# Opening of a two-block transformer kernel: inputs loaded first, modulation and first convolution group in pairs of K-blocks, modulation sums in halves

## The chip, the cores and the metric

The program runs on one core of one Trainium2 chip. The metric is the device time of one execution in microseconds, taken as a median over runs. The engines are TensorE (PE, with its weight loads as PEld), VectorE (DVE), ScalarE (ACT), GpSimd (POOL), and SyncE (SP), whose queue issues the loads from memory.

## The reference

Two transformer blocks of two layers each run one after the other on a sequence of 256 tokens of width 1024, in 32-bit floats. The change is in the first layer of the first block. There a modulation vector is computed from a conditioning vector, for the tokens (`c`) and for a context of 256 rows (`c_ctx`), then the normalised tokens are scaled and shifted by it and go through a short convolution:

```python
mod = jax.nn.silu(c) @ w_ada[i] + b_ada[i]
mod_c = jax.nn.silu(c_ctx) @ w_ada[i] + b_ada[i]
sh1, sc1, g1, sh2, sc2, g2 = jnp.split(mod[:, None, :], 6, axis=-1)
...
h = _modulate(_rms_norm(x, norm_mix[i]), sh1, sc1)
hc = _modulate(_rms_norm(ctx, norm_mix[i]), sh1c, sc1c)
...
b_gate, c_gate, u = jnp.split(h @ w_in, 3, axis=-1)
z = c_gate * u
...
zc = sum(conv_w[j] * zp[:, j:j + n] for j in range(CONV_WIDTH))
return (b_gate * zc) @ w_out
```

`_modulate(h, shift, scale)` is `h * (1 + scale) + shift`. `w_ada` has 6 pieces of 1024 columns for each layer. The shift and the scale of the first normalisation (pieces 0 and 1) are needed before the first matmul of the convolution, piece 2 after it, and pieces 3 and 4 ahead of the feed-forward net.

## The kernel before, in words

Activations lie transposed, 1024 features as 8 K-blocks of 128 partitions, and tokens and context side by side as 512 columns. To keep 32-bit precision on a faster matmul type, every operand is split into a high part and a rest, and a product is three matmuls (`mm3`, L240 to L245): high by high, high by rest, rest by high. ACT writes the high part of a weight (L106) and DVE the rest (L107).

All weights come through one stream (`WeightStream`, L57): a list of units of at most 128 x 1024 elements, loaded in order by SP (L90) into five raw buffers, split two units ahead of use into four pairs of buffers. A load can only start when the unit five places ahead in the list has left its buffer. Units marked raw are not split but used as they are.

Engines take instructions in their program order. A scheduler fixes that order when the program is built, with its own estimate of durations, so an instruction that waits holds all that stands behind it on its engine.

The opening (`conv_block`) does this. Sums of squares of the tokens (X) and of the context (C) give a reciprocal root by Newton steps (`diagonal`, L347 to L786), which is spread over partitions by a matmul with ones (L791); `normalise` writes `xr` (L793). The shift and scale pieces are computed in four chunks of 512 columns, each over all 8 K-blocks: two with raw weights (`ada_direct`, matmul L454, row copy L459, transposes L440) and two with split weights (`ada_fast`, matmuls L417 and L418, row copy L423, transposes L427). Chunks 0 and 2 hold the first halves of shift and scale. With them `modulate(0)` (L802, then split at L251 and L252) makes K-blocks 0 to 3 of the convolution's input, and the first convolution matmuls (L243 to L245) run on them; the other two chunks give K-blocks 4 to 7.

The convolution has four groups g of 256 features, each with three products c, u and b of 48 K-block steps, that is 144 matmuls of 512 columns. A group's results are combined by DVE and ACT (L853 to L861). Meanwhile the later modulation pieces run on DVE: each unit of 128 x 1024 weights is multiplied by the conditioning value of its partition and added to an accumulator, once for the tokens and once for the context (L473, L475). After 8 units a piece is summed over partitions: PE transposes the accumulators into auxiliary PSUM banks (L483), DVE reduces each bank (L485). There are three auxiliary banks, and a piece for two vectors needs four. `ADA_UNITS` says how many units are taken at which step.

Of the kernel before, what the change touches and what calls it, by code (L numbers as in the profile page):

```python
# [140 lines left out]
def ada_units(w, j, raw):  # L141
    return cols_units(w, j * 512, 512, list(range(8)), raw)


# [21 lines left out]
class Net:  # L166
    def __init__(self, tc, a, out, es):
# [11 lines left out]
        self.banks(5, 3)  # L179
# [3 lines left out]
        nc.sync.dma_start(self.kc, a["consts"])  # L183
# [5 lines left out]
        self.X = self.cp.tile([P, KB, T], F32, name="X")  # L189
        self.mod = self.cp.tile([P, 2, 48, 2], F32, name="mod")  # L190
        self.modA = self.cp.tile([P, 4, KB, 2], F32, name="modA")


# [203 lines left out]
    def ada_start(self):  # L397
        nc = self.nc
        sil = self.sil = self.cp.tile([P, 16], F32, name="sil")
        self.ada_plan = AdaPlan()  # L400
        self.ada_pending = []
        nc.scalar.activation(sil, self.pk[:, 0:16], AF.Silu)
# [5 lines left out]
    def ada_fast(self, layer, j):  # L408
# [3 lines left out]
        done = 0  # L412
        while done < KB:
            hi, lo, nk, _ = self.ws.take()
            for kk in range(nk):
                kb = done + kk
                nc.tensor.matmul(ps[0:4, :], self.c4[:, kb, :], hi[:, kk, :], start=kb == 0, stop=False)  # L417
                nc.tensor.matmul(ps[0:4, :], self.c4[:, kb, :], lo[:, kk, :], start=False, stop=kb == KB - 1)  # L418
            done += nk
            if done < KB:  # L420
                yield
        row = self.tmp()
        nc.scalar.copy(row[0:4, :], ps[0:4, :])  # L423
        yield
        pt = self.aux_bank()
        for b in range(4):
            nc.tensor.transpose(pt[:, 4 * b : 4 * b + 4], row[0:4, b * P : (b + 1) * P], self.ident[0:4, 0:4])  # L427
        m = self.mod[:, layer, 4 * j : 4 * j + 4, :]
        bias = self.p(f"b_ada{layer}")[:, 4 * j : 4 * j + 4, None].to_broadcast([P, 4, 2])
        col = self.small(16, "ada_col")  # L430
        nc.vector.tensor_copy(col, pt[:, :16])
        cv = col.rearrange("p (b v s) -> p b v s", b=4, v=2)
        nc.vector.tensor_tensor(m, cv[:, :, :, 0], cv[:, :, :, 1], ALU.add)
        nc.vector.tensor_tensor(m, m, bias, ALU.add)

    def ada_columns(self, layer, j, row):

        pt = self.aux_bank()
        for b in range(4):
            self.nc.tensor.transpose(pt[:, 2 * b : 2 * b + 2], row[0:2, b * P : (b + 1) * P], self.ident[0:2, 0:2])  # L440
        bias = self.p(f"b_ada{layer}")[:, 4 * j : 4 * j + 4, None].to_broadcast([P, 4, 2])
        m = self.mod[:, layer, 4 * j : 4 * j + 4, :]
        self.nc.vector.tensor_tensor(m, pt[:, :8].rearrange("p (b v) -> p b v", b=4), bias, ALU.add)

    def ada_direct(self, layer, j):

        nc = self.nc
        ps = self.aux_bank()
        sil = self.sil.rearrange("p (v k) -> p k v", v=2)
        done = 0  # L450
        while done < KB:
            w, _, nk, _ = self.ws.take()
            for kk in range(nk):
                nc.tensor.matmul(ps[0:2, :], sil[:, done + kk, :], w[:, kk, :], start=done + kk == 0, stop=done + kk == KB - 1)  # L454
            done += nk
            if done < KB:
                yield
        row = self.tmp()
        nc.scalar.copy(row[0:2, :], ps[0:2, :])  # L459
        yield  # L460
        self.ada_columns(layer, j, row)

    def ada_slow(self, layer, j, vecs):
# [13 lines left out]
        yield  # L477
        col = self.small(16, "ada_sum")
        for v in range(vecs):
            for h in range(2):  # L480
# [4 lines left out]
                nc.vector.tensor_reduce(col[:, o : o + 4], pt.rearrange("p (b k) -> p b k", b=4), AX.X, ALU.add)  # L485
        bias = self.p(f"b_ada{layer}")[:, 8 * j : 8 * j + 8, None].to_broadcast([P, 8, vecs])
        nc.vector.tensor_tensor(self.mod[:, layer, 8 * j : 8 * j + 8, 0:vecs], col[:, : 8 * vecs].rearrange("p (v b) -> p b v", b=8), bias, ALU.add)

    def ada_at(self, *step):
        self.ada_pending = [g for g in self.ada_pending if next(g, WAIT) is None]  # L490
        for layer, j, kb in self.ada_plan.at(step):
            if kb == 0:
                self.ada_piece = self.ada_slow(layer, j, ada_vecs(layer, j))
            next(self.ada_piece)
            if kb == KB - 1:
                self.ada_pending.append(self.ada_piece)

    def ada_flush(self):
        for g in self.ada_pending:
            for _ in g:  # L500
                pass
        self.ada_pending = []

    def mod_scale(self, layer, which, half):

        nv = 2 - layer * which
        hs = slice(4 * half, 4 * half + 4)
        g = self.p(("norm_mix" if which == 0 else "norm_ffn") + str(layer))[:, hs, None].to_broadcast([P, 4, nv])
        sc = self.mod[:, layer, (3 * which + 1) * 8 + 4 * half : (3 * which + 1) * 8 + 4 * half + 4, 0:nv]
# [161 lines left out]
ADA_FIRST = (0, 2, 1, 3)  # L671
ADA_DIRECT = (0, 2)
# [26 lines left out]
def stream_specs(a):  # L699
# [3 lines left out]
    for i in range(2):  # L703
        s += ada_units(w[0], ADA_FIRST[i], ADA_FIRST[i] in ADA_DIRECT)
    for k0 in (0, 4):
        for c0 in (1024, 2048):
            s += cols_units(a["conv_w_in"], c0, 256, k8[k0 : k0 + 4])
# [1238 lines left out]
```

## Time and profile before

| what | before |
|---|---|
| median of 3 runs | 2047.08 us (2044.90 to 2047.14) |
| the profiled execution | 2047.39 us, span 2045.6 us, mean granted clock 0.995 |
| PE busy | 2009.8 us, 98% of the span |
| DVE busy | 1497.8 us, 73% |
| ACT busy | 1026.5 us, 50% |
| memory read | 345.68 MB, 170 GB/s over the span |

Times within the execution are microseconds from the start of the span. A row of the timeline gives start, duration, engine, source line, operation, tiles written and read, how many instructions were merged, and in brackets how long the engine was idle before and what ended that. Successive matmuls overlap in the records, so what a matmul costs is the distance between two starts, not its duration. One matmul in 32-bit floats shows as two records. A row of windows gives the stretch, its length, busy time with the count of instructions for PE, PEld, DVE, ACT and POOL, then the granted clock of PE, the busy share of the DMA engines and GB/s; where only one tile's or one line's instructions are asked for, engines that have none are left out.

### The profile page before, as it was taken

How to read it: one execution, taken by the hardware profiler on the slowest of the kernel's cores; microseconds unless marked ns; L12 is line 12 of the kernel's file. 1: busy time of each engine (PE TensorE's matmuls, PEld its weight loads, DVE VectorE, ACT ScalarE, POOL GpSimd, SP SyncE). 2: the span in 40 equal slices, each digit the busy share in tenths (PEclk: the TensorE clock that was granted, in tenths of full speed). 3: DMA queues.
4: the chain of work that ended last, by engine and by line, in shares of the span. 5: the costliest groups of instructions: out<-in, count | busy, mean ns of one | idle time of the engine just before them, and what ended most of it. 6: DMA issues, size and time to landing. Idle time of an engine off the chain costs nothing. (4 is left out here: it accounts for less than half of the span.)

```text
span 2045.6 us, 31905 instructions
## 1 busy us (share of the span) xinstructions
PE 2009.8 (98%) x12318; PEld 1769.8 (87%) x12318; DVE 1497.8 (73%) x2632; ACT 1026.5 (50%) x1684; POOL 4.1 (0%) x24
## 2 busy tenths in 40 slices
PE   7999999999999999999999999999999999999999
PEld 3778988888899999888888899998888888989888
DVE  5996777777577779766677767787767776887764
ACT  4432533223355556655455546655545554675552
POOL 0000000000000000000000000000000000000000
PEclk8999999999999999999999999999999999999999
DMA  7773365577454334565566564556556656425554
GB/s 242 237 215 120 118 190 180 170 235 248 126 178 133 91 98 131 155 188 187 181 187 194 177 189 126 158 171 194 181 185 191 190 180 186 135 83 171 186 180 134
DMA packets 315080, 348.82 MB, mean 171 GB/s; under 512 B 12528, under 2 KB 299376, under 8 KB 314928
## 3 DMA queue, kind: packets, MB, share of 16 engines
q1 hardware_dynamic: 314928, 346.78, 54.9%
q8 instruction: 97, 1.59, 0.3%
q14 instruction: 55, 0.45, 0.1%
HBM read 345.68 MB, written 1.05 MB: 170 GB/s over the span
## 5 line engine op out<-in xcount | busy, mean ns | idle before, releaser
L106 ACT CAST whi<-wraw 128x512 fp32r<-128x512 f32 (+1 forms) x777 | 608.2, 804 | 738.8 <-issue 192.4
L107 DVE TENSOR_TENSOR wlo<-wraw,whi 128x512 fp32r<-128x512 f32 (+1 forms) x777 | 702.0, 918 | 366.3 <-ACT whi L106 362.0
L306 PE MATMUL pg<-x,whi 128*128 128x512 f32 x1408 | 386.9, 396 | 0.5 <-DVE x L255 0.4
L306 PEld LDWEIGHTS pg<-x,whi 128*128 128x128 f32 x1408 | 239.5, 188 | 34.2 <-DVE x L255 2.2
L306 PE MATMUL po<-s,whi 128*128 128x512 f32 x880 | 243.0, 394 | 0.0
L308 PEld LDWEIGHTS pg<-x,wlo 128*128 128x128 f32 x1408 | 213.9, 188 | 32.4
L308 PE MATMUL pg<-x,wlo 128*128 128x256 f32 x1408 | 221.0, 279 | 0.0
L243 PE MATMUL pm<-xh,whi 128*128 128x512 f32 (+1 forms) x576 | 218.3, 382 | 0.8 <-ACT xh L251 0.8
L244 PE MATMUL pm<-xl,whi 128*128 128x512 f32 (+1 forms) x576 | 219.0, 381 | 0.0
L245 PE MATMUL pm<-xh,wlo 128*128 128x512 f32 (+1 forms) x576 | 218.5, 380 | 0.0
L475 DVE SCALAR_TENSOR_TENSOR ada_acc<-wraw,sil,ada_acc 128x1024 f32<-128x1024 f32 x112 | 140.6, 1280 | 33.5 <-DMA wraw<-in_w_ada 33.1
L306 PEld LDWEIGHTS po<-s,whi 128*128 128x128 f32 x880 | 148.7, 189 | 18.1
L308 PEld LDWEIGHTS po<-s,wlo 128*128 128x128 f32 x880 | 137.5, 188 | 20.5
L308 PE MATMUL po<-s,wlo 128*128 128x256 f32 x880 | 142.5, 280 | 0.0
L243 PEld LDWEIGHTS pm<-xh,whi 128*128 128x128 f32 x576 | 109.3, 190 | 21.9 <-ACT xh L251 1.5
L245 PEld LDWEIGHTS pm<-xh,wlo 128*128 128x128 f32 x576 | 109.3, 190 | 20.8
L244 PEld LDWEIGHTS pm<-xl,whi 128*128 128x128 f32 x576 | 109.3, 190 | 20.4 <-issue 0.2
L243 PE MATMUL pm<-sh,whi 128*128 128x256 f32 (+1 forms) x352 | 113.8, 323 | 0.0
L245 PE MATMUL pm<-sh,wlo 128*128 128x256 f32 (+1 forms) x352 | 113.6, 323 | 0.0
L244 PE MATMUL pm<-sl,whi 128*128 128x256 f32 (+1 forms) x352 | 113.3, 322 | 0.0
L245 PE MATMUL pm<-whi,xl 128*128 128x256 f32 x352 | 99.6, 283 | 0.0
L306 PE MATMUL pg<-xh,whi 128*128 128x512 f32 x352 | 96.1, 394 | 1.9 <-DVE xh L252 1.9
(431 smaller groups left out, 3390.5 us busy)
## 6 DMA issues: line engine op xcount, KB each, us to landing
wraw<-in_ffn_w_in SPq DMA_DIRECT2D x264, 512.0 KB, 3.6
wraw<-in_ffn_w_out SPq DMA_DIRECT2D x128, 512.0 KB, 3.6
wraw<-in_w_ada SPq DMA_DIRECT2D x96, 512.0 KB, 4.5
wraw<-in_a_w_in SPq DMA_DIRECT2D x28, 512.0 KB, 3.8
wraw<-in_conv_w_in SPq DMA_DIRECT2D x24, 512.0 KB, 4.7
wraw<-in_attn_w_qkv SPq DMA_DIRECT2D x24, 512.0 KB, 4.0
wraw<-in_ffn_w_out SPq DMA_DIRECT2D x28, 256.0 KB, 2.9
wraw<-in_b_w_in SPq DMA_DIRECT2D x14, 512.0 KB, 3.9
```

Source lines behind the costliest of these rows:

```text
L106: self.nc.scalar.copy(hi[:, cs], raw[:, cs])
L107: self.nc.vector.tensor_tensor(lo[:, cs], raw[:, cs], hi[:, cs].bitcast(F32), ALU.subtract)
L243: mm(ps, ah, bh, start=first, stop=False)
L244: mm(ps, ah, bl, start=False, stop=False)
L245: mm(ps, al, bh, start=False, stop=last)
L306: self.nc.tensor.matmul(pss[c], hi[:, kk, cs], x2[:, done + kk], start=done + kk == 0, stop=False)
L308: self.nc.tensor.matmul(pss[c][:, 0, :], lo[:, kk, cs], x2[:, done + kk, 0, :], start=False, stop=done + kk == nblocks - 1)
L475: nc.vector.scalar_tensor_tensor(accs[v], w, c, accs[v], ALU.mult, ALU.add)
```

## The change

- **Loads.** X is loaded second, right behind the small parameters (`pack`), then C, then the constants, then five units of the weight stream. Before, the constants came first and two weight units stood between X and C.
- **Statistics.** Tokens and context share one run of the Newton steps (4 columns at once). Squares are taken in turn by ACT and DVE, and their sums over partitions are accumulated by small matmuls as they come.
- **Added matmuls.** 28 matmuls of ones by a constant (`warm`), whose results are not used, stand ahead of and between the statistics.
- **Chunks.** A chunk i now holds 256 columns of the shift and 256 of the scale, for K-blocks 2i and 2i+1 alone (`ada_parts`). Chunks 0 and 1 use raw weights, 2 and 3 split ones; the total of columns is the same.
- **First convolution group.** It runs by pairs of K-blocks: for each pair, c, u and b one after the other, into six open PSUM banks (six main and two auxiliary banks up to here, then five and three as before). The weights of this group come in units of 128 x 512 instead of 128 x 1024. Chunk i+1 is computed behind c of pair i, its transposes stand between the two halves of u, and the modulation of the next pair follows.
- **Units and sums.** The four units of later modulation pieces that ran with group 0 are gone from there, group 3 ends with one unit instead of two, and five now run with the output projection of the convolution (`conv_out`). A piece's sum is taken at most two banks at a step and two or more steps after its last unit.

```diff
-        self.banks(5, 3)
+        self.banks(6, 2)
...
     def ada_at(self, *step):
-        self.ada_pending = [g for g in self.ada_pending if next(g, WAIT) is None]
+
+        self.ada_step += 1
+        for _ in range(2):
+            if self.ada_pending and self.ada_pending[0][0] <= self.ada_step - 2:
+                self.ada_sum()
...
-ADA_UNITS = {("conv", 0, 2): 4}
-ADA_UNITS.update({("conv", g, n): 3 if n == 2 and g < 3 else 2 for g in range(1, 4) for n in range(3)})
+ADA_UNITS = {("conv", g, n): 3 if n == 2 else 2 for g in range(1, 4) for n in range(3)}
+ADA_UNITS["conv", 3, 2] = 1
+ADA_UNITS.update({("conv_out", g): 3 - g for g in range(2)})
...
+    ada = [[u for c1 in (0, 1024) for u in cols_units(w[0], c1 + i * 256, 256, k8, i < ADA_RAW)] for i in range(4)]
+    s += ada[0]
+    for i in range(4):
+        for n, c0 in enumerate(CONV_COLS):
+            s += cols_units(a["conv_w_in"], c0, 256, k8[2 * i : 2 * i + 2])
+            if n == 0 and i < 3:
+                s += ada[i + 1]
...
+    net.load_halves(net.X, net.a["xT"])
     net.load_halves(net.C, net.a["ctxT"])
+    nc.sync.dma_start(net.kc, net.a["consts"])
+    net.ws.load(5)
+    pcu = [[net.main_bank() for _ in range(2)] for _ in CONV_COLS]
+    warm(16)
+    dg = diagonals()
...
+    for i in range(4):
+        ada = None
+        for n, pss in enumerate(pcu):
+            hi, lo, nk, _ = net.ws.take()
+            for c in range(2):
...
+                    net.mm3(pss[c], hi[:, kk, cs], lo[:, kk, cs], xh[:, kb, :], xl[:, kb, :], kb == 0, kb == KB - 1)
+                if n == 1 and c == 0 and ada is not None:
+                    for _ in ada:
+                        pass
+                    modulate(i + 1)
+            if n == 0 and i < 3:
+                ada = net.ada_parts(i + 1)
+                for _ in range(3):
+                    next(ada)
```

Three places in the built order matter to the prediction.

First, PE at the opening. Before (whi and wlo are the two parts of a weight, xh and xl those of the convolution's input, pa an auxiliary and pm a main PSUM bank, kc the constants, c_104 the split conditioning vector): all of the raw chunks (L454) stand ahead of the first convolution matmul (L243).

```order
L454 MATMUL pa<-wraw,sil 2x512 x4
L791 MATMUL pa<-t,ones 128x256
L361 MATMUL pa<-mean,acc 128x1 x4
L454 MATMUL pa<-wraw,sil 2x512 x4
L791 MATMUL pa<-t,ones 128x256
L454 MATMUL pa<-wraw,sil 2x512 x8
L440 MATMUL pa<-kc,t 128x2 x8
L417 MATMUL pa<-whi,c_104 4x512
L418 MATMUL pa<-wlo,c_104 4x512
L417 MATMUL pa<-whi,c_104 4x512
L418 MATMUL pa<-wlo,c_104 4x512
L243 MATMUL pm<-xh,whi 128x512 x4
```

The same place now (a raw chunk's matmul is L429 and has 256 columns, its transposes are L439, the convolution is L242 to L244, L849 spreads the reciprocal root):

```order
L429 MATMUL pa<-wraw,sil 2x256 x8
L849 MATMUL pa<-t,ones 128x256 x2
L429 MATMUL pa<-wraw,sil 2x256 x8
L439 MATMUL pa<-kc,t 128x2 x4
L429 MATMUL pa<-wraw,sil 2x256 x7
L242 MATMUL pm<-xh,whi 128x512 x2
L429 MATMUL pa<-wraw,sil 2x256
L243 MATMUL pm<-xl,whi 128x512
```

One chunk with its transposes, and seven matmuls of the next, now stand ahead of the first convolution matmul; the second half of that next chunk (8 more L429) follows after the 12 matmuls of c of the first pair, then come 6 of u, the four transposes of chunk 1, and the other 6 of u.

Second, ACT at the second modulation. Before, behind the first raw chunk's row copy:

```order
L459 COPY t<-pa 2x512
L106 CAST whi<-wraw 128x512 x5
L459 COPY t<-pa 2x512
L106 CAST whi<-wraw 128x512
L802 ACTIVATE t<-xr,mod,modA 128x256 x3
```

Now, behind the first chunk's row copy (L435; L853 keeps the reciprocal root, L833 scales and shifts):

```order
L106 CAST whi<-wraw 128x512
L853 COPY acc<-pa 128x512
L435 COPY t<-pa 2x512
L833 ACTIVATE t<-xr,mod,modA 128x256 x2
L250 CAST xh<-t 128x512 x2
L106 CAST whi<-wraw 128x512 x5
L435 COPY t<-pa 2x512
L833 ACTIVATE t<-xr,mod,modA 128x256 x3
```

Five weight casts stand ahead of the row copy of chunk 1 as they stood ahead of the second row copy before. By the numbers of the buffers the last two of the five are the two halves of one unit of 128 x 1024, the first unit of chunk 2.

Third, PE at a piece's sum. Before, in group 2 of the convolution, twelve transposes (three banks), four matmuls, and four transposes (the fourth bank):

```order
L483 MATMUL pa<-kc,ada_acc 128x128 x12
L243 MATMUL pm<-xh,whi 128x512
L244 MATMUL pm<-xl,whi 128x512
L245 MATMUL pm<-xh,wlo 128x512
L243 MATMUL pm<-xh,whi 128x512
L483 MATMUL pa<-kc,ada_acc 128x128 x4
L244 MATMUL pm<-xl,whi 128x512
```

Now the same piece's sum stands in two places, each of eight transposes (two banks), 48 convolution matmuls apart; the first of them:

```order
L244 MATMUL pm<-xh,wlo 128x512
L470 MATMUL pa<-kc,ada_acc 128x128 x8
L242 MATMUL pm<-xh,whi 128x512
```

A sum of the first feed-forward net that stood as 12, one matmul, 4 (around 350 us) is split in the same way. The sum late in `conv_out` (now 12, one matmul, 4; before 12, two matmuls, 4) and the two sums during the feed-forward output (12, two matmuls, 4) keep that form. From the feed-forward net's first output on, the order on every engine is the same as before.

More of the change, by code (lines that the diff above doesn't have):

```diff
@@ L776, in units, with warm @@
+    def warm(n):
         for _ in range(n):
[L777 to L794 removed]
@@ L887, in conv_block @@
+        conv_pool.close()
         state = {}
```

333 lines of the change are left out of this document (170 added, 163 removed).

## The prediction

> **What bounds the kernel now.** I read the page first, then the windows of the opening, then the timeline of PE, and last that of ACT and DVE around PE's gaps.
>
> ```profile
> PE 2009.8 (98%) x12318; PEld 1769.8 (87%) x12318; DVE 1497.8 (73%) x2632; ACT 1026.5 (50%) x1684; POOL 4.1 (0%) x24
> ```
>
> PE is busy 98% of the span, so a gain must come from the 2% in which it is idle or from time in which it works slowly. The windows (PE, PEld, DVE, ACT, POOL, then granted clock, DMA share, GB/s) show where both lie:
>
> ```profile
> 0.00:20.00 20.00, 9.24 (x28) 4.06 (x29) 10.14 (x31) 6.40 (x12) 0.20 (x4) 1.00 0.88 292
> 20.00:40.00 20.00, 15.55 (x43) 4.85 (x42) 11.57 (x31) 8.72 (x17) 0.00 (x0) 0.84 0.80 258
> ...
> 12.00:14.00 2.00, 2.00 (x5) 0.75 (x6) 1.13 (x7) 1.15 (x2) 0.00 (x0) 1.00 1.08 372
> ...
> 34.00:36.00 2.00, 1.34 (x7) 0.71 (x7) 1.38 (x4) 1.38 (x4) 0.00 (x0) 0.50 0.94 314
> ...
> 38.00:40.00 2.00, 2.00 (x5) 1.61 (x6) 1.19 (x2) 2.00 (x5) 0.00 (x0) 0.50 0.81 298
> ...
> 42.00:44.00 2.00, 2.00 (x7) 1.55 (x6) 2.00 (x4) 1.94 (x4) 0.00 (x0) 0.52 0.04 8
> ...
> 130.00:132.00 2.00, 2.00 (x6) 1.51 (x6) 2.00 (x5) 0.00 (x0) 0.00 (x0) 0.50 0.78 237
> ```
>
> PE lacks 10.8 us of the first 20 and 4.5 of the next, and from 34 to 44 it runs at a clock of 0.5. PE's timeline gives the chain:
>
> ```profile
> 10.76 1.86 PE L361 MATMUL pa<-mean,acc 128*128 128x1 f32 x8 [10.76 <-DVE acc L352]
> ...
> 24.60 7.03 PE L454 MATMUL pa<-wraw,sil 128*2 128x512 f32 x16
> ...
> 34.66 0.58 PE L440 MATMUL pa<-kc,t 2*128 2x2 f32 x4 [2.70 <-ACT t L459]
> ...
> 37.88 2.07 PE L243 MATMUL pm<-xh,whi 128*128 128x512 f32 x4 [0.84 <-ACT xh L251]
> ...
> 129.00 0.91 PE L483 MATMUL pa<-kc,ada_acc 128*128 128x128 f32 x4 [1.92 <-DVE ada_sum L485]
> ...
> 350.31 0.66 PE L483 MATMUL pa<-kc,ada_acc 128*128 128x128 f32 x4 [1.68 <-DVE ada_sum L485]
> ```
>
> The convolution starts at 37.88. The gap of 2.70 ahead of the transposes (L440) is ACT's doing, as its timeline shows:
>
> ```profile
> 33.51 0.62 ACT L106 CAST whi<-wraw 128x512 fp32r<-128x512 f32 x1 [1.33 <-DMA wraw<-in_w_ada]
> 34.04 0.57 ACT L459 COPY t<-pa 2x512 f32<-2x512 f32 x1
> ```
>
> The row copy's input was there when the raw chunk ended (31.6), but a cast that waited for its load stood ahead of it. When group 0 ends is read from a count, the tile pm alone (PE, PEld, DVE, ACT):
>
> ```profile
> 0.00:80.95 80.95, 37.65 (x144) 28.94 (x145) 1.15 (x2) 1.17 (x2) 0.94 0.76 247
> 81.00:124.40 43.40, 43.40 (x193) 35.95 (x192) 4.10 (x7) 1.75 (x3) 1.00 0.69 216
> ```
>
> The 144th convolution matmul starts by 80.95, and behind it 192 to 193 take 43.40 us, 0.226 each, without a hole. So E, the end of group 0, is the point to forecast; what E gains, the whole kernel gains, as long as PE stays full behind it.
>
> **Part by part: inputs first.** The loads' rows on ACT, and two of the page's rows on time to landing:
>
> ```profile
> 8.55 1.15 ACT L347 ACTIVATE t<-X 128x512 f32<-128x512 f32 x2 [0.28 <-DMA X<-in_xT]
> ...
> 14.18 1.15 ACT L347 ACTIVATE t<-C 128x512 f32<-128x512 f32 x2 [0.34 <-DMA C<-in_ctxT]
> ```
>
> ```profile
> wraw<-in_ffn_w_out SPq DMA_DIRECT2D x128, 512.0 KB, 3.6
> wraw<-in_w_ada SPq DMA_DIRECT2D x96, 512.0 KB, 4.5
> ...
> wraw<-in_ffn_w_out SPq DMA_DIRECT2D x28, 256.0 KB, 2.9
> ```
>
> C was complete at 14.18 behind 0.34 MB of constants and two weight units of 0.52 MB. Without these 1.38 MB, at the 372 GB/s of the window from 12 to 14, it is there 3.7 us sooner, at 10.5; the constants and chunk 0's four units (2.4 MB more) at 17.0. A square and two adds (about 0.7 each on DVE) and the small matmuls put the statistics at 13.0. The 28 added matmuls fill PE while it waits for X and C, so they cost nothing, unless they run into the statistics; they should leave PE's clock full for chunk 0.
>
> Chunk 0: 16 records of L454 take 7.03 us, 0.44 each; a matmul of 512 columns is two, so one of 256 columns costs about 0.44. Eight from 13.0 end at 16.5. The Newton steps and the diagonal are ready at 15.8 (in the trace 2.6 us behind the statistics), two L849 at about 0.45 end at 17.4, eight more L429 at 20.9. Row copy 0.6, four transposes 0.5: 22.1. From there I take the trace's chain:
>
> ```profile
> 35.28 0.17 DVE L443 TENSOR_TENSOR mod<-pa,pk 128x8 f32<-128x8 f32 x1 [0.42 <-PE pa L440]
> ...
> 35.74 1.58 ACT L802 ACTIVATE t<-xr,mod,modA 128x256 f32<-128x256 f32 x3 [0.62 <-DVE modA L510]
> 37.23 0.60 ACT L251 CAST xh<-t 128x512 fp32r<-128x512 f32 x1
> ```
>
> From 35.28 to the first matmul at 37.88 it is 2.6; DVE has one `normalise` (0.6) more between, so the first convolution matmul starts at 25.3, against 37.88.
>
> **What PE has left until E.** 144 matmuls at 0.226: 32.5. Raw ones, 9 at 0.44: 4.0. Split chunks, 64 of 256 columns, at the distance of
>
> ```profile
> 210.13 0.28 PE L243 MATMUL pm<-sh,whi 128*128 128x256 f32 x1
> 210.25 0.28 PE L244 MATMUL pm<-sl,whi 128*128 128x256 f32 x1
> ```
>
> 0.12: 7.7. Transposes, three times 0.45: 1.4. In all 45.6, so E is 70.9 without a wait.
>
> **The waits.** They are at the three handovers from a chunk to the next pair. At the first, the row copy of chunk 1 stands on ACT behind the two casts of chunk 2's first unit. That unit's load takes the buffer of chunk 1's third unit, which PE has read after 12 convolution matmuls and five raw ones, at 25.3 + 2.7 + 2.2 = 30.2. Landing 4.5 later (taken from `w_ada`'s row; 3.6 and 5.4, the median of `w_ada` in the first 60 us, are the ends), 34.7; casts 1.1 and copy 0.6 with signals: 36.5. PE is at the transposes at 25.3 + 2.7 + 4.0 + 1.4 = 33.4. It waits 3.1, between 2.2 and 4.0. Behind the copy on ACT's queue stands the modulation of the next pair, so that is late too.
>
> ```profile
> wraw<-in_w_ada SPq DMA_DIRECT2D x20, 512.0 KB, 5.4
> ```
>
> After the waits of 2.70 and 1.92 above the clock fell to 0.5, from 129.5 to about 133 the second time, 3.5 us; after 1.68 it did not. So I add half of 3.5 us, 1.7. The Trainium skill, TensorE: Matmul & The Clock Gate, section Why this matters for your kernels, asks for no idle gap over about 3 us; by that, a wait of 2.2 would leave the clock alone and E would be 1.7 sooner, but this trace fell at 1.92, so the rows decide.
>
> At the other two handovers the unit whose cast stands ahead of the copy needs a split buffer that PE frees by the chunk's own last matmul, so it is late by about one cast, 0.6 each. Waits in all 6.0 (2 to 11). E = 76.9, a gain of 4.0 (8 to -1).
>
> The smaller loads of group 0, twelve of 256 KB for six of 512, land in 2.9 against 3.6 by the page's rows; one after the other that is 13.2 us more, side by side at the 372 GB/s nothing. Five are in flight, so I take nothing. DMA: Bandwidth & Descriptors, section Rules for kernel authors, in the Trainium skill, wants 1 MiB per load; its fit of 2.0 us plus bytes over 436 GB/s, an estimate of 2.6 and 3.2 us, would give 12 us here in place of 13.2.
>
> **Sums in halves.** At 129 PE waited because DVE was still in accumulations:
>
> ```profile
> 124.68 3.66 DVE L475 SCALAR_TENSOR_TENSOR ada_acc<-wraw,sil,ada_acc 128x1024 f32<-128x1024 f32 x3
> ...
> 128.27 2.47 DVE L485 TENSOR_REDUCE ada_sum<-pa 128x4 f32<-128x512 f32 x4
> ...
> 130.14 0.63 PE L245 MATMUL pm<-xh,wlo 128*128 128x512 f32 x1
> ...
> 130.57 0.63 PE L243 MATMUL pm<-xh,whi 128*128 128x512 f32 x1
> ```
>
> With two banks at a time and three there, no transpose waits for a reduce. That is 1.9, and the matmuls behind it at 0.43 in place of 0.226, seven of them, 1.4: 3.3. The split sum at 350 gives 1.7. The remaining (12, one, 4) late in `conv_out` may wait up to 1.9 at a place where DVE is less full; I take 0.
>
> **DVE's units.** DVE is the second engine here, and E comes sooner for it:
>
> ```profile
> 140.00:160.00 20.00, 20.00 (x90) 16.57 (x89) 19.99 (x22) 6.56 (x9) 0.00 (x0) 1.00 0.66 197
> 160.00:180.00 20.00, 20.00 (x98) 16.64 (x97) 12.31 (x15) 4.47 (x5) 0.00 (x0) 1.00 0.49 150
> L475 DVE SCALAR_TENSOR_TENSOR ada_acc<-wraw,sil,ada_acc 128x1024 f32<-128x1024 f32 x112 | 140.6, 1280 | 33.5 <-DMA wraw<-in_w_ada 33.1
> ```
>
> A unit is two of these, 2.56. From E to the end of group 3 DVE has 19 units (48.6), 18 splits at 1.2 (22), the combining of nearly four groups (about 7 each, 26) and six reduces (4): 100 us against 432 matmuls, 98, and 16 transposes, 2, on PE. Before, it was 24 units in about 110 us, and only the sum made PE wait. Five units, 12.8 us, now lie in the stretch that was at 12.31 of 20. I take 0.
>
> **Sum.** 4.0 + 3.3 + 1.7 = 9.0 from the profiled execution's 2047.4 (span 2045.6 and 1.8 around it, 0.3 above the median of the runs): 2038.4.
>
> **The rivals.**
> - *The handovers are hidden* (loads land in 3.6 or less, and E is 72): 8.9 + 5.0, 2033.5. For it: DMA is near idle when that unit is called. Against it: the same row of casts made PE wait 2.70 before.
> - *Every handover waits like the first* (three times 3.4, E about 81): the opening gains nothing, the sums' 5.0 stay, 2042.4.
> - *The sums gain nothing*: DVE at 100 of 100 us falls behind, and PE waits for a weight's rest or a bank instead; 4.0 alone, 2043.4.
> - *Slower, by a cold PE.* Each of the three handovers repeats what the one before cost: 2.70 idle, and 34 to 44 at half clock, about 4.2 us lost of 8.5 busy. Three times 6.9 on 70.9 is E = 91.6, 10.7 later, less 5.0: 2053.1. It needs gaps near 2.7 at all three and thin PE work behind each. Against it: behind the transposes 18 matmuls stand ready, where the trace had few.
>
> **How the numbers follow.** Forecast 0.52 (2035 to 2041), handovers hidden 0.20, every handover waits 0.12, sums gain nothing 0.11, slower 0.05. About 0.2%, 4 us, is what a measurement here tells from no change: the first three are faster (0.84), the fourth lies on the edge and counts as the same, the last is slower. The range runs from the second, with 2 off for a sooner start, to the third and part of the fourth: 2031.5 to 2043.
>
> **What would show it.** Right: first convolution matmul near 25, 144th near 77, a PE gap of about 3 at the transposes of chunk 1 released by the row copy and a clock of 0.5 behind it, no PE wait for `ada_sum` in group 2 or near 340. Wrong: a first matmul beyond 28, a second or third gap of that size, PE waiting for `wlo` or a bank behind E, or group 0 ending by 73.

## The result and the profile after

| what | before | after |
|---|---|---|
| median of four runs | 2046.09 us (2044.90 to 2047.14) | 2033.11 us (2032.77 to 2035.45) |
| ratio | | 0.9939, 95% interval 0.9922 to 0.9956 |
| the profiled execution | 2047.39 us, span 2045.6 | 2032.84 us, span 2031.0 |
| mean granted clock | 0.995 | 0.999 |

The change took 13.0 us off by the medians. The forecast was 2038.4 with a range from 2031.5 to 2043.0: the time is inside the range and the sign is right, but it is 5.3 us below the forecast and at the number of the first rival (handovers hidden, 2033.5). In gain that is 9.0 forecast against 13.0; the other 1.3 us come from starting at the profiled execution of the kernel before, which was slower than its median. A second group of runs of the changed kernel, below, has the ratio 0.9948 (0.9935 to 0.9961), 10.9 us by its medians.

The windows of the opening of the kernel after (PE, PEld, DVE, ACT, POOL, clock, DMA share, GB/s), and the stretch in which PE waited for a sum before:

```profile
0.00:20.00 20.00, 18.67 (x116) 14.78 (x117) 10.11 (x31) 5.76 (x12) 1.20 (x6) 1.00 0.91 286
20.00:40.00 20.00, 19.34 (x88) 10.89 (x87) 11.74 (x23) 10.87 (x21) 0.00 (x0) 1.00 0.76 240
...
120.00:140.00 20.00, 20.00 (x94) 16.65 (x93) 17.76 (x18) 4.13 (x5) 0.00 (x0) 1.00 0.69 218
```

The clock column is 1.00 in all three, where it was down to 0.84 in the second before. PE's waits in the first 620 us (engine, tile and line, who released it, us in total, times, longest) show what is left:

```profile
PE pm L784 <- DVE mean L184: 1.2, 1, 1.2
PE pa L360 <- DVE acc L551: 0.8, 1, 0.8
PE pa L439 <- ACT t L435: 0.7, 1, 0.7
```

These are the three longest; two more are 0.2 each. No wait for a sum, none for a weight, and of the row copies (L435) only chunk 0's. PE's timeline, chunk 0 to the transposes of chunk 1, and ACT's rows that answer to it:

```profile
13.68 3.62 PE L429 MATMUL pa<-wraw,sil 128*2 128x256 f32 x16
17.22 1.13 PE L849 MATMUL pa<-t,ones 128*128 128x256 f32 x4
18.28 3.62 PE L429 MATMUL pa<-wraw,sil 128*2 128x256 f32 x16
22.56 0.40 PE L439 MATMUL pa<-kc,t 2*128 2x2 f32 x4 [0.67 <-ACT t L435]
22.90 3.19 PE L429 MATMUL pa<-wraw,sil 128*2 128x256 f32 x14
26.01 0.73 PE L242 MATMUL pm<-xh,whi 128*128 128x512 f32 x2
...
34.82 0.41 PE L439 MATMUL pa<-kc,t 2*128 2x2 f32 x4
```

```profile
10.26 0.63 ACT L794 ACTIVATE t<-C 128x512 f32<-128x512 f32 x1 [0.86 <-DMA C<-in_ctxT]
...
32.77 1.14 ACT L106 CAST whi<-wraw 128x512 fp32r<-128x512 f32 x2 [2.14 <-DMA wraw<-in_w_ada]
33.81 0.57 ACT L435 COPY t<-pa 2x512 f32<-2x512 f32 x1
```

The row at 34.82 has no bracket. The forecast put 3.1 us of idle time and a cold clock there. The row copy does stand behind the two casts of chunk 2's first unit, as the prediction says, but that unit was there at 32.77 and not at 34.7.

E is read from the count of the tile pm. Behind it stand the two groups of pm that are not convolution, 56 and 32 records:

```profile
0.00:73.00 73.00, 47.63 (x232) 38.25 (x233) 1.58 (x4) 1.16 (x2) 1.00 0.78 249
```

```profile
L784 PE MATMUL pm<-mean,ones 128*128 128x128 f32 x56 | 9.2, 334 | 1.2 <-DVE mean L184 1.2
...
L802 PE MATMUL pm<-mean,t 128*128 128x1 f32 x32 | 3.8, 246 | 0.1
```

232 less 88 are 144, so E is 73.0, against 80.95 before: 7.9 sooner.

**A clean mark for the experiments.** GpSimd's first memset behind the opening (`bias`, 128 x 256) marks the start of the next layer. Its rows, before and after:

```profile
623.88 0.31 POOL L988 MEMSET bias<- 128x256 f32 x1 [623.44 <-DVE t L533]
```

```profile
610.41 0.32 POOL L1038 MEMSET bias<- 128x256 f32 x1 [608.69 <-DVE t L531]
```

It comes 13.5 us sooner. From windows of 10 us each I add up PE's idle time and the time lost to a lower clock (one less the clock, times 10) ahead of the mark and behind it:

| up to 610 us | before | after |
|---|---|---|
| PE idle | 19.1 | 3.5 |
| lost to the clock | 6.9 | 0.0 |
| PE busy with the 28 added matmuls | 0 | 9.2 |

15.6 and 6.9 less 9.2 are 13.3, against 13.5 at the mark. That it closes so well is partly luck. The kernel before is idle for another 0.8 us between 610 and its own mark, and its first matmuls were slow by 2.0 us that the clock column does not show (see *Without the added matmuls*). With both the sum is 16.1, and 2.6 us of additional time on PE in the kernel after are not accounted for.

Behind the mark the two programs do the same work, yet the profiled executions part by another 1.1 us there. Windows of the kernel after show what differs between executions:

```profile
1216.00:1218.00 2.00, 2.00 (x18) 1.78 (x18) 1.85 (x7) 1.00 (x3) 0.00 (x0) 0.88 0.75 242
1218.00:1220.00 2.00, 2.00 (x12) 1.21 (x10) 1.28 (x8) 0.00 (x0) 0.00 (x0) 0.50 0.25 26
1220.00:1222.00 2.00, 2.00 (x16) 1.68 (x15) 0.38 (x4) 0.00 (x0) 0.00 (x0) 0.77 0.69 236
```

PE is busy throughout, and the clock is at half for about 3.4 us, which loses 1.7 (0.12, 0.50 and 0.23 of 2 us each). Before has that stretch and a second near 1748. Over the fourteen profiled executions of this study the loss behind 610 us lies between 1.7 and 6.8 us, mostly in steps of 1.7, whatever the kernel. The kernel before had medians of 2046.1, 2044.4, 2046.2 and 2043.9 in the four groups of runs, the last three on different chips. So the mark, ahead of those places, is the finer measure here; but it is read from one execution of each kernel, and only that of the kernel after was repeated.

### The profile page after: what moved, and what is told of

Its sections match the earlier page's. It is cut to its first block, busy times and chain, and to the rows that moved or that the text cites. A ratio compares the mean times of both kernels' runs of the same rounds, so it can differ in the third digit from the quotient of the medians.

```text
span 2031.0 us, 32187 instructions
## 1 busy us (share of the span) xinstructions
PE 2011.6 (99%) x12454; PEld 1778.8 (88%) x12454; DVE 1496.3 (74%) x2626; ACT 1024.7 (50%) x1681; POOL 5.1 (0%) x26
## 3 DMA queue, kind: packets, MB, share of 16 engines
HBM read 345.68 MB, written 1.05 MB: 171 GB/s over the span
## 5 line engine op out<-in xcount | busy, mean ns | idle before, releaser
L242 PE MATMUL pm<-xh,whi 128*128 128x512 f32 (+1 forms) x576 | 217.8, 380 | 0.2 <-ACT xh L250 0.2
L243 PE MATMUL pm<-xl,whi 128*128 128x512 f32 (+1 forms) x576 | 217.4, 378 | 0.0
L244 PE MATMUL pm<-xh,wlo 128*128 128x512 f32 (+1 forms) x576 | 217.4, 378 | 0.0
L243 PEld LDWEIGHTS pm<-xl,whi 128*128 128x128 f32 x576 | 108.4, 188 | 20.6 <-DVE xl L251 0.9
L242 PEld LDWEIGHTS pm<-xh,whi 128*128 128x128 f32 x576 | 108.1, 188 | 20.8 <-ACT xh L250 1.0
L244 PEld LDWEIGHTS pm<-xh,wlo 128*128 128x128 f32 x576 | 108.3, 188 | 19.9
L242 PE MATMUL pm<-sh,whi 128*128 128x256 f32 (+1 forms) x352 | 113.9, 324 | 0.0
L244 PE MATMUL pm<-sh,wlo 128*128 128x256 f32 (+1 forms) x352 | 113.6, 323 | 0.0
L243 PE MATMUL pm<-sl,whi 128*128 128x256 f32 (+1 forms) x352 | 113.3, 322 | 0.0
L244 PE MATMUL pm<-whi,xl 128*128 128x256 f32 x352 | 99.6, 283 | 0.0
```

What stands on the lines that cost most here:

```text
L242: mm(ps, ah, bh, start=first, stop=False)
L243: mm(ps, ah, bl, start=False, stop=False)
L244: mm(ps, al, bh, start=False, stop=last)
```

## The experiments

All kernels ran beside the kernel before. "Mark" is the memset's time in the profiled execution (610.3 for the kernel after, mean of two), the ratio is to the kernel before.

| kernel | mark, us | ratio, 95% interval |
|---|---|---|
| before | 623.9 | 1 |
| after, again | 610.2 | 0.9948 (0.9935 to 0.9961) |
| sums whole again | 620.2 | 1.0006 (0.9997 to 1.0016) |
| before, with sums in halves | 617.9 | 0.9974 (0.9965 to 0.9984) |
| one raw buffer held | 610.4 | 0.9962 (0.9950 to 0.9974) |
| one foreign transfer | 614.6 | 0.9966 (0.9953 to 0.9978) |
| old order of loads | 612.5 | 0.9968 (0.9957 to 0.9980) |
| before, with new order of loads | 620.0 | 1.0001 (0.9992 to 1.0010) |
| without the added matmuls | 614.1 | 0.9958 (0.9944 to 0.9971) |
| units at their old places | 613.0 | 0.9975 (0.9965 to 0.9985) |
| chunk 1 split | 608.7 | 0.9947 (0.9934 to 0.9960) |
| chunk 1 half split | 609.2 | 0.9975 (0.9965 to 0.9985) |
| and chunk 0 half split | 612.5 | 0.9972 (0.9963 to 0.9981) |

**The kernel after, once more.**

> The changed kernel once more, beside the others of this call, since executions of one kernel differ by 2 to 5 us. Both theories: median near 2032 to 2035, ratio to the kernel before 0.993 to 0.996; the 256-column memset that marks the start of attention (POOL, first one behind the opening) near 610.4; the granted clock dips to 0.5 for about 3.5 us near 1218 or near 1732 in some executions, 1.7 us each, without a PE wait over 0.3 ahead of it.

Mark, waits and span (2031.0) repeat to 0.2 us; the median was 2035.28. C was complete at 11.22 here and at 10.26 in the first execution, and yet the first convolution matmul came at 26.08 and 26.01.

### The handover that did not wait

**One raw buffer held.** Edit of the kernel after:

```diff
-    net.ws.load(5)
+    held = net.ws.raw_pool.tile([P, WeightStream.UNIT], F32, name="wraw", tag="raw")
+    nc.gpsimd.memset(held[:, 0:8], 0.0)
+    net.ws.load(4)
...
         evict(0, 2)
+        nc.gpsimd.tensor_tensor(net.small(8, "held"), held[:, 0:8], zs[0][:, 0, 1:9], ALU.add)
```

> The changed kernel with one of the five raw weight buffers kept occupied until group 0 is evicted, so that chunk 2's first unit is asked for later (behind the split of c02's weights instead of c01's, an estimate of 35 to 36 instead of 29.0). Theory (the row copy of a chunk stands on ScalarE behind the casts of the next chunk's first unit, and the forecast failed only in when that unit is asked for): that unit lands at 39 or later, PE waits 4 to 7 us at chunk 1's transposes, the granted clock falls to about 0.5 behind it, and E comes at 80 to 84 instead of 73.1: time 2040 to 2044, ratio 0.997 to 0.999. Rival (the handover doesn't hang on that unit; PE or the scheduler's order hides it whenever it lands): no PE wait over 1.5 us there, clock 1.0, time within 2 us of 2033.1.

The theory's wait did not come, but the run does not decide between the two. The unit was asked for at 30.96 instead of 28.98, and the scheduler, which knows the buffers, now put the row copy ahead of its cast. ACT's timeline of this kernel:

```profile
32.94 0.57 ACT L435 COPY t<-pa 2x512 f32<-2x512 f32 x1 [0.51 <-PE pa L429]
34.42 0.62 ACT L106 CAST whi<-wraw 128x512 fp32r<-128x512 f32 x1 [0.92 <-DMA wraw<-in_w_ada]
```

So the order in which copy and casts stand follows the scheduler's own estimate of the load. It can only wait for a lateness that the scheduler doesn't foresee.

**One foreign transfer.** That is what this edit makes: a load of 2.1 MB that nothing reads, on GpSimd's queue. The order of ACT, PE and SP stays as it was.

```diff
     modulate(0)
+    nc.gpsimd.tensor_copy(extra[:, 0:8], xr[:, 2, 0:8])
+    nc.gpsimd.dma_start(extra.rearrange("p (a c) -> p a c", c=1024), net.a["w_ada"][1][0:512, 0:1024].rearrange("(a p) c -> p a c", p=P))
```

> The changed kernel with one transfer of 2.1 MB that nothing reads, from another queue, when chunk 1 has been normalised (near 25). All engines keep their order of instructions, so chunk 1's row copy still stands behind the two casts of chunk 2's first unit. Theory (the wait that was forecast is there as soon as that unit lands later than 33.3): at 372 GB/s the transfer takes 5.6 us of the loads' share, the unit lands 3 to 5.6 later, at 36 to 38, PE waits 2 to 5 us at chunk 1's transposes or just ahead of them for c01's or c02's weights, the clock falls to 0.5 for about 3.5 us behind it, and E and the memset at 610.4 come 4 to 7 later: time 2037 to 2040, ratio 0.996 to 0.998. Rival (the handover has slack that the forecast overlooked, or the other queue's transfer doesn't slow the weights): PE waits under 1 us in all, the memset within 1 us of 610.4.

The theory held, in all its numbers but the moment of the transfer (issued at 22.48, not near 25). ACT, PE, and the windows behind:

```profile
36.04 1.14 ACT L106 CAST whi<-wraw 128x512 fp32r<-128x512 f32 x2 [0.79 <-DMA wraw<-in_w_ada]
37.08 0.57 ACT L435 COPY t<-pa 2x512 f32<-2x512 f32 x1
```

```profile
37.71 0.41 PE L439 MATMUL pa<-kc,t 2*128 2x2 f32 x4 [2.37 <-ACT t L435]
```

```profile
38.00:40.00 2.00, 2.00 (x9) 1.61 (x9) 0.33 (x2) 1.45 (x3) 0.00 (x0) 0.80 0.91 267
40.00:42.00 2.00, 2.00 (x7) 1.52 (x6) 1.00 (x2) 2.00 (x5) 0.00 (x0) 0.50 0.99 341
42.00:44.00 2.00, 2.00 (x9) 1.67 (x8) 1.59 (x3) 0.88 (x3) 0.00 (x0) 0.85 0.45 155
```

From the landing to the transposes it is 1.67 us. PE waits 2.37, the clock loses 1.7 (0.20, 0.50 and 0.15 of 2 us each), and the mark is 4.3 later. (The first convolution matmul was at 26.47 already, 0.4 later than in the kernel after.) In the kernel after PE reaches the transposes at 34.82, so any landing up to 33.15 is free, and it was 32.77: 0.4 us of slack.

The Trainium skill, TensorE: Matmul & The Clock Gate, section Why this matters for your kernels, allows idle gaps up to about 3 us; here 2.37 already lowered the clock, and so did 1.92 in the kernel before. A gap of 1.48 (chunk 1 split, below) did not. Smaller gaps than these did so elsewhere, in some executions only; the last section has them.

### The sums

**Sums whole again.** The two lines that let a sum pause between banks are gone from the kernel after:

```diff
-                if v < vecs - 1 or h == 0:
-                    yield
```

> The changed kernel with one part undone: each sum of a modulation piece is again made whole in one go, all its banks of transposes and reduces in a row. Theory (the sums in halves bring 3.3 at group 2 and 1.7 near 340): PE waits again for a reduce, 1.9 in group 2 and about 1.7 at a later sum, the clock falls to 0.5 behind the first, and the kernel takes 3 to 5 us more than the changed one: 2036 to 2038, ratio to the kernel before 0.995 to 0.9965. Rival (the halves bring nothing, the pieces only fall at better places now): no PE wait for a sum over 0.5 us and a time within 1 us of 2033.1, ratio 0.994; then the whole 13 us would be the opening's.

The kind of wait was right and the size wrong by a factor of two: the mark is 9.9 later, all of the gain but 3.6, and by the medians nothing of the gain is left. PE and DVE (lines are two lower in this kernel):

```profile
138.92 1.47 PE L470 MATMUL pa<-kc,ada_acc 128*128 128x128 f32 x12
140.14 0.48 PE L242 MATMUL pm<-xh,whi 128*128 128x512 f32 x1
146.07 1.11 PE L470 MATMUL pa<-kc,ada_acc 128*128 128x128 f32 x4 [5.45 <-DVE ada_sum L472]
```

```profile
144.73 0.68 DVE L875 TENSOR_TENSOR t<-pm,t 128x512 f32<-128x512 f32 x1
145.34 1.28 DVE L472 TENSOR_REDUCE ada_sum<-pa 128x4 f32<-128x512 f32 x2
```

The last four transposes need a bank that a reduce must empty, and that reduce stands on DVE behind the eviction of group 2 (L875). PE waits 5.45 and then works until 151.7 at half clock. In halves, the same transposes come a step later and nothing waits.

**The kernel before, with sums in halves.** The edit is the new `ada_at`, `ada_sum` and `ada_slow` of the change, nothing else.

> The kernel before with one part of the change alone: the sums of the modulation pieces go in halves. Theory (the prediction's terms): the PE waits of 1.92 near 129 and 1.68 near 350 go and so does the half clock behind the first, 3.3 + 1.7 = 5.0 us: the memset at 623.9 comes at 618.9, ratio 0.9970 to 0.9982. Rival (the halves pay for what the spread of the units puts in their way, so alone they bring little; whole sums cost 9.8 us in the changed kernel because the units had moved): gain 0 to 2 us, memset at 622 to 624, ratio 0.999 to 1.000; PE then still waits for a sum or a bank somewhere else.

The theory held: no wait for a sum is left, the median is 5.2 us lower (2040.94 to 2046.16), the mark 6.0 sooner. So 5.0 was the right price for the halves in the old program; in the new one, where the units have moved, whole sums would cost twice that.

**Units at their old places.** The kernel after with the old table of units, sums in halves:

```diff
-ADA_UNITS = {("conv", g, n): 3 if n == 2 else 2 for g in range(1, 4) for n in range(3)}
-ADA_UNITS["conv", 3, 2] = 1
-ADA_UNITS.update({("conv_out", g): 3 - g for g in range(2)})
+ADA_UNITS = {("conv", 0, 2): 4}
+ADA_UNITS.update({("conv", g, n): 3 if n == 2 and g < 3 else 2 for g in range(1, 4) for n in range(3)})
```

> The changed kernel with the modulation units where they were before: four behind group 0's last evictions, none in the second convolution, sums still in halves. Theory (once sums go in halves, the units' places don't matter, VectorE has room for them): no PE wait over 1 us in groups 1 to 3, the memset that marks the start of attention within 1 us of 610.3, time within 2 us of the changed kernel. Rival (whole sums cost 9.8 us in the changed kernel, so VectorE's queue is near its limit there, and where the units lie decides): four units more by the end of group 0, 10 us of VectorE, make PE wait 2 to 6 us for a sum, a bank or a split of weights in groups 1 and 2, with half clock behind it; memset at 613 to 619, ratio to the kernel before 0.996 to 0.999.

Between the two: the mark is 2.7 later, with no half clock and no wait for a sum. Group 0's 144th matmul started by 74.2, and of the two waits one lies ahead of it and one, over the 1 us that the theory allowed, at the start of group 1. PE, and what DVE did meanwhile:

```profile
66.42 0.50 PE L243 MATMUL pm<-xl,whi 128*128 128x512 f32 x1 [0.95 <-DVE xl L251]
...
77.64 0.50 PE L244 MATMUL pm<-xh,wlo 128*128 128x512 f32 x1 [1.40 <-DVE wlo L107]
```

```profile
67.49 3.67 DVE L463 SCALAR_TENSOR_TENSOR ada_acc<-wraw,sil,ada_acc 128x1024 f32<-128x1024 f32 x3
```

Units that DVE takes between 62 and 71 delay the split of the inputs and of the next weights. Moving them out of group 0 is worth these 2.7 us.

### The loads and the added matmuls

**Old order of loads.** The kernel after, with constants, X, two units, C, three units:

```diff
+    nc.sync.dma_start(net.kc, net.a["consts"])
     net.load_halves(net.X, net.a["xT"])
+    net.ws.load(2)
     net.load_halves(net.C, net.a["ctxT"])
-    nc.sync.dma_start(net.kc, net.a["consts"])
     net.ws.load(5)
```

> The changed kernel with the order of the first loads as it was before: constants, X, two weight units, C, three weight units. Theory (C sets the statistics and these set everything until E): C lands 3.7 us later, near 14, the raw matmuls of chunk 0 start near 17.2 instead of 13.7, first convolution matmul near 29.5 instead of 26.0, E near 76.6, time 3 to 4 us more: 2036 to 2037, ratio 0.995 to 0.996. Rival (the units of chunk 0 land sooner in exchange and the second half of the raw chunk catches up): first convolution matmul by 27, time within 1 us of 2033.1.

The rival's first sign came, a first convolution matmul at 26.69, and half of the theory's price: the mark is 2.1 later, since four more records of raw matmuls now stand behind that first matmul and PE waits 0.6 more for row copies. C was complete at 15.18, 4.9 later than in the kernel after (3.7 to 5.3 later than in all executions with the new order), but the scheduler let PE do eight of chunk 0's raw matmuls ahead of C's statistics, as two of its units were there.

**The kernel before, with the new order of loads.**

```diff
-        nc.sync.dma_start(self.kc, a["consts"])
...
-    net.ws.load(2)
     net.load_halves(net.C, net.a["ctxT"])
+    nc.sync.dma_start(net.kc, net.a["consts"])
+    net.ws.load(2)
```

> The kernel before with the order of the first loads alone changed: X, C, constants, then units. Theory (C sets the statistics, as the prediction's step has it): C lands 3.7 sooner, first convolution matmul near 34.2 instead of 37.9, the memset near 620.2 instead of 623.9, ratio 0.9978 to 0.9988. Rival (what is gained on C is lost on the weight units that now stand behind it; the old order cost the changed kernel 1.5 to 2.0 only): first convolution matmul at 36 to 38, memset at 622 to 624, ratio 0.999 to 1.000.

The rival held by the medians, and for its reason: C came at 10.95, but PE then waited for a unit, and the convolution began at 39.62, later than the 37.88 before and than the rival's 36 to 38.

```profile
13.27 6.41 PE L453 MATMUL pa<-wraw,sil 128*2 128x512 f32 x8 [1.24 <-DMA wraw<-in_w_ada]
...
39.62 2.07 PE L242 MATMUL pm<-xh,whi 128*128 128x512 f32 x4 [0.68 <-ACT xh L250]
```

The mark (620.0) lands on the theory's 620.2 all the same, by luck, because in this execution PE waited 0.9 for the sums instead of 3.6 and kept its clock there. Whether other executions of the kernel before do so too was not seen: there is one profile of it. The loads alone bring nothing that eleven runs can tell.

**Without the added matmuls.** `warm` does nothing:

```diff
-            nc.tensor.matmul(pcu[0][0][:, :P], net.ones, net.mean, start=True, stop=True)
+            pass
```

> The changed kernel without its 28 matmuls on constants, whose results nothing uses. Theory (they keep the clock full for chunk 0's raw matmuls): the granted clock is 0.5 when chunk 0 starts, its first eight take 2.0 to 3.6 us more, the first convolution matmul comes near 28 to 29 instead of 26.0, and so do E and the memset at 610.4, 2 to 3 later: time 2035 to 2037. Rival (the statistics' own matmuls warm the clock, or the chain through VectorE covers it): first convolution matmul within 0.7 of 26.0, the memset within 0.7 of 610.4, time within 1 us of the changed kernel.

The theory held in its mechanism: first convolution matmul at 29.05 (3.0 later), mark 3.8 later, where 2 to 3 was expected. But the clock column does not show it, and chunk 0's first eight matmuls take 1.5 more, not 2.0 to 3.6; the other half of the 3.0 comes ahead of them, where the statistics' one-column matmuls are slow too (the first eight records take 1.87 instead of 1.05). PE's rows and the window around chunk 0:

```profile
9.99 5.28 PE L802 MATMUL pm<-mean,t 128*128 128x1 f32 x24 [1.22 <-DVE t L798]
15.20 5.13 PE L429 MATMUL pa<-wraw,sil 128*2 128x256 f32 x16
...
21.32 3.62 PE L429 MATMUL pa<-wraw,sil 128*2 128x256 f32 x16
```

```profile
14.00:16.00 2.00, 2.00 (x8) 1.39 (x9) 0.75 (x5) 0.00 (x0) 0.00 (x0) 1.00 1.10 349
```

The first 16 records of chunk 0 take 5.13, the second 16 take 3.62, and the column says 1.00. The Trainium skill, TensorE: Matmul & The Clock Gate, section Part 1: The HAM clock gate, has PE at half rate by default until some 3.4 us of sustained work; by that the start is cold, and the durations here agree, while the column does not. Nor were the 5.2 us of one-column matmuls ahead of chunk 0 enough: two to three records start in each half microsecond up to about 18, and four from there on. The kernel before paid for it too: its first eight records of L454 took 5.60, the next eight 3.60.

### Less work on PE

From 23 us on PE has no wait over 0.2 until E, so less work should bring E sooner. Three kernels test that: chunk 1 split like chunks 2 and 3 (`ADA_RAW = 1`); its second half alone split, with four stationary columns for the raw half; and chunk 0's second half split as well. The edits of the last two, with the set of raw halves of the half split:

```diff
-ADA_RAW = 2
+ADA_RAW = {(0, 0), (0, 1), (1, 0)}
...
-        raw = i < ADA_RAW
-        sil = self.sil.rearrange("p (v k) -> p k v", v=2)
+        raw = (i, 0) in ADA_RAW and (i, 1) in ADA_RAW
+        sil = self.sil.rearrange("p (v k) -> p k v", v=2) if raw else self.sil4
...
-                    if raw:
+                    if lo is None:
```

> The changed kernel with chunk 0 alone multiplied raw; chunk 1 is split into two halves like chunks 2 and 3. Theory (in the opening PE's own work sets E, as no wait is left): the 32 matmuls of 0.226 of chunk 1, 7.2 us, become 32 of 0.12, 3.9 us, and E comes 3.3 us sooner, near 69.8: time near 2030, ratio 0.992. Rival (ScalarE and VectorE set the pace as soon as PE has less to do: four units more to cast and to subtract, 1.1 and 1.4 us each, in the stretch from 22 to 34, ahead of the first group's weights): PE waits 2 to 5 us for a split of chunk 1 or of the first weights, perhaps at half clock behind it, and the time is 2033 to 2038.

> The changed kernel with chunk 0 raw as it is and chunk 1 half raw, half split (its second half's two units are cast and subtracted, and its raw half has four stationary columns, two of them zero). Theory (PE has no wait from 26 on, so E is the sum of its work, as long as the split half's casts lie in ScalarE's idle 28 to 33): 16 matmuls of 0.226 become 16 of 0.12, 1.7 us off PE, no new wait over 0.5, the memset near 608.6. Rival (splitting all of chunk 1 saved 3.4 of work and brought 1.7, and the rest went into waits of 3.0 in the first 40 us; half of it makes a wait just as well): memset at 610 to 611, the time within 1 us of the changed kernel.

> As the one before, and chunk 0's second half is split too. Theory (its two units land by 17 at the latest and ScalarE is idle from 11 to 16, so their casts hide behind the first half's matmuls): 3.4 us off PE's work in all, first convolution matmul near 24.5 instead of 26.0, the memset near 607. Rival (chunk 0 lies on the chain of latencies to the first modulation, not on PE's work; casts and differences come behind the landing, and VectorE is in the Newton steps): PE waits 1 to 3 us at chunk 0's second half or its transposes, memset at 609 to 612.

With chunk 1 split the mark is 1.6 sooner, half of the 3.3: PE's idle time in the first 100 us grew from 2.2 to 4.3: 0.8 at chunk 0's transposes, where the row copy now stands behind two more casts, 0.8 for the first split inputs (`xh`) and 0.5 for a weight's rest.

```profile
22.69 0.40 PE L439 MATMUL pa<-kc,t 2*128 2x2 f32 x4 [1.48 <-ACT t L435]
```

With half of it split the mark is 1.1 sooner of 1.7. Neither shows in a ratio. Chunk 1 split has 0.9947, no other than the 0.9948 of the kernel after, but on another chip; half split has 0.9975, by which it would be slower, from a chip on which the kernel after did not run. So neither can be set beside it. With chunk 0 split the mark is 2.1 later. PE waited little, but the clock fell, at a place without a gap:

```profile
12.00:14.00 2.00, 2.00 (x21) 1.99 (x20) 0.84 (x2) 0.00 (x0) 0.00 (x0) 1.00 1.10 348
14.00:16.00 2.00, 2.00 (x6) 0.58 (x6) 1.63 (x11) 0.00 (x0) 0.00 (x0) 0.51 1.10 348
```

The clock fell once more near 25 us, behind waits of only 0.67 and 0.27. In all, 3.4 us are lost to the clock in the opening of this execution. So no version here is shown to beat the kernel after.

## Why the prediction was right in sign and too small in size

The step that failed is the term of the waits at the three handovers, put at 6.0 (2 to 11) and measured at 0.0. The prediction's own signs say so: no gap at chunk 1's transposes, no half clock behind them, and group 0 ended by 73, which it had named as a sign of being wrong. That 2033.1 lies inside the range is owed to the rival that the range took in, not to the sum.

| step of the prediction | forecast | measured |
|---|---|---|
| C complete | 10.5 | 10.26 |
| chunk 0's raw matmuls start | 13.0 | 13.68 |
| first convolution matmul | 25.3 | 26.01 |
| PE's work from there to E | 45.6 | 47.0 |
| waits at the handovers | 6.0 | 0.0 |
| E | 76.9 | 73.0 |
| sums in halves | 5.0 | 5.2 (median), 6.0 (mark) |
| DVE's units, moved | 0 | 2.7 (mark) |
| smaller loads | 0 | 0, no wait for a weight |
| gain in all | 9.0 | 13.0 (medians), 13.5 (mark) |

Of the 13.5 at the mark, 7.9 lie ahead of E and 5.6 behind it, against 4.0 and 5.0 in the sum. So the shortfall is in the opening: the 6.0 of waits that did not come, less a start that was 0.7 later and 1.4 more work, are the 3.9 that were missing there.

**The first handover.** That a late unit makes PE wait there was right: the foreign transfer brought the wait, the half clock and a loss of 4.3 us. What was wrong is which instruction releases the load. The three times were each a little off, all the same way. The unit was asked for at 28.98 and not at 30.2: the prediction took the buffers in list order, so that this unit followed chunk 1's third, which PE reads. Five units are in flight, but in the built order this load waits for DVE and not for PE: it takes the buffer of the first pair's u, free when DVE had split off its second part. SP's row, and its wait in the stretch from 28.9 to 29.1:

```profile
28.98 3.32 SPq L90 DMA_DIRECT2D wraw<-in_w_ada  x4
```

```profile
SPq L90 <- DVE wlo L107: 1.2, 1, 1.2
```

It was there 3.8 later and not 4.5. And PE was at the transposes at 34.82 and not at 33.4, since the start was 0.7 later and the work ahead of it longer. 1.2, 0.7 and 1.4 make 3.3 us, against a wait of 3.1. The forecast varied only the second of these, the time to landing, for its range from 2.2 to 4.0; what that difference of nearly equal times could really be began below nothing, and the lower end of the waits (2) should have been 0. The other two handovers had no wait either.

**The loads and the added matmuls** were costed as a chain: C sooner, so everything sooner. The times came out within 0.8, but the reason was too short. C itself varies more than that: with the same order of loads it was complete between 9.89 and 11.46 in the nine executions with the added matmuls, and the first convolution matmul moved less, between 25.60 and 26.47 (the last kernel, with its half clock, left out). The new order of loads alone does nothing that the medians show for the kernel before, and in the kernel after it is worth 2.1 at the mark. The 28 matmuls, put at nothing, did cost nothing and are worth 3.8 by what they save: the prediction took the full rate for chunk 0's first eight matmuls, which needs them, without a price for it. The rest of the opening's 7.9 us, 2.0 if the parts add up, is left to running by pairs, so that one chunk and not two stand ahead of the first convolution matmul; that part was not tried by itself.

**The sums** were priced right for the old program (5.0 to 5.2). As parts of the new one they are worth 9.9, since there a whole sum meets a fuller DVE queue. **The units** were put at 0 with the reason that DVE has room; the room that mattered was around the end of group 0.

The rivals: *handovers hidden* is what happened, at its number, though for the reason above more than for faster loads. *Every handover waits* and *slower, by a cold PE* did not occur; the foreign transfer shows that one late unit would have given back 4.3 us. The price of the first of these two was also mis-summed: the first handover was put at 3.1 of wait and 1.7 of clock, so three like it are 14.4 and not three times 3.4. *The sums gain nothing* is refuted by the kernel before with sums in halves.

## What to carry to other kernels

A wait worked out as the difference of two times, each read to about 1 us, has a range that begins at nothing: keep the zero in. When a scheduler sets the order and hands out buffers, read from the built order which instruction releases each load, and remember that an edit may move the very instruction it is meant to delay. Before costing a part of a change at nothing, ask what the others rest on it for: here chunk 0's rate rested on the added matmuls, and undoing the halves in the new program cost twice what they had brought in the old one.

## What the runs showed of the hardware

- PE's start is slow for some microseconds while the granted clock column reads 1.00. Without the added matmuls chunk 0's first 16 records take 0.32 us each; with them the same records take 0.226. Durations tell, the column doesn't.
- The clock went to half behind every gap of 1.92 us and more that was seen after the start (1.92, 1.93, 2.37, 2.47, 2.70 and 5.45), and not behind single ones of 1.40, 1.48 and 1.68. That is no threshold. Every kernel has a gap of 1.73 or 1.74 near 840 us and one of 1.31 or 1.32 near 1800; half clock followed the first in 4 of the 14 executions and the second in 5. The first of them without a fall behind it (kernel after) and with one (kernel before, sums in halves):

```profile
833.29 0.74 PE L305 MATMUL pg<-xh,whi 128*128 128x512 f32 x2 [1.73 <-DVE xh L251]
```

```profile
840.86 1.14 PE L306 MATMUL pg<-xh,whi 128*128 128x512 f32 x2 [1.73 <-DVE xh L252]
```

- It also went to half for about 3.4 us where PE had no gap at all: between 1216 and 1232 in 11 of the 14 executions, between 1732 and 1747 in 6, and at 14 us in the last kernel. Each of these places lies just behind a run of one-column matmuls (L360 and L1310 of the kernel after, from 1215.09 to 1217.24; 16 records in 1.84 us in the last kernel). So one-column work may count as little as a gap does, as at the start without the added matmuls, but no run tests it: the kernel after has the same 16 records ahead of its chunk 0 without a fall, and what decides stays open.
